# The factor of the norm ahead of an MLP, applied as its square behind the second matrix

## The chip, the core and the metric

The kernel runs on one core of a Trainium2 chip. The metric is the device time of one execution, in microseconds (us); lower is better. The engines are TensorE (PE; its weight loads are listed as PEld), VectorE (DVE), ScalarE (ACT), GpSimd (POOL) and SyncE (SP); the last two issue most of the DMAs here.

## The reference

One decoder layer on 16 meta tokens and 256 tokens of width 2048, all in fp32. The change works in the last third, the MLP, and what matters of it is:

```python
h = h + rms_norm(m @ w_o[l], g_post_mix[l])
u = rms_norm(h, g_pre_mlp[l])                           # h * r * g, r = rsqrt(mean(h*h) + eps) per token
f = jnp.square(jax.nn.relu(u @ w_up[l])) @ w_down[l]    # 2048 -> 8192 -> 2048
h = h + rms_norm(f, g_post_mlp[l])
```

The factor r is one positive number per token. It passes through the first matrix and the relu as a factor and through the square as its square. So f with r is f without r, times r*r, token by token.

## The kernel before

Ahead of the MLP come the mixers (some 500 us). The MLP starts at about 527 us of the span. A weight matrix is not multiplied as it is: each block of 128x2048 numbers ("raw") is cast by ScalarE to a coarser high part ("hi", line 1907), VectorE subtracts that from the block to get the low part ("lo", line 1912), and TensorE multiplies high by high, high by low and low by high. hi and lo stand in three buffers each, in turn, so the cast for a product can start when the product three places ahead of it has ended. Raw blocks come by DMA from SP's queue into seven places ("rooms").

The 8192 hidden columns are worked off in eight pieces. What TensorE does in a piece is a row of words written by hand:

- U0a0 to U1b1 are products with w_up (eight a piece, 32 matmuls each, in pairs of 512 and 256 columns; lines 551 and 557). The first digit is the half of the piece, the letter the pair of 128 columns in it, the last digit the half of the inner dimension. A pair ends in the PSUM banks u0 and u1, which every pair uses. A + means that the product belongs to the next piece.
- P1 to P7 and Q1 to Q7 are products with w_down (12 matmuls of 512 columns each, line 2082), in a scheme of seven products for eight blocks, on the left half of the output columns (P) and on the right one (Q). X1 to X4 are plain products in the last piece.
- R, in the first piece alone, stands for the broadcast of r: two fp32 matmuls of a matrix of ones with a diagonal (rows2, line 1969) give r along the free dimension, which VectorE copies to the tile rb.

After a pair of U products, up_pair reads the banks out (half on ScalarE, line 1980, the sum of halves on VectorE, line 1987, both 128x256). relu_squared then makes max(s, 0) * rb on VectorE (line 2007, 128x512), the square on ScalarE (line 2012), the sums of forms (lines 2023 to 2033) and their high and low parts (lines 2041 to 2059), which are the stationary side of the P and Q products. Work of piece 0 that needs rb waits in a list until R.

Some products want a sum of two w_down blocks (ADDS_FOR, eight a piece with forms). PIECE_SUMS says which of these VectorE adds up from two loaded blocks (line 1924, a 128x2048 addition, before the split). The others are "brought": POOL issues a DMA that adds the second block onto the first one in SBUF as it loads it (line 1929). There are 24 of the first kind and 36 of the second. give (line 2111) adds a finished P or Q product from its bank to the totals F and G.

The order of all other engines' work is set by a planner (Plan.order): TensorE's row is fixed, every other piece of work has a cost written by hand and gets a due time from the product that needs it, and each engine takes the work that is ready and due first. Each engine then runs its list in order.

At the end the sums of squares of the outputs are taken on ScalarE as the last columns come (square_of, line 1582, square_half, line 2361), end_norm makes the factor of the last norm, and finish_down multiplies, adds h and sends the result off:

```python
nc.scalar.activation(r, ssq, AF.Abs_reciprocal_sqrt, bias=v, scale=-4.0 / D)
minus4_mean(q, t, ssq)
between()
nc.vector.scalar_tensor_tensor(v, r, q, r, op0=ALU.mult, op1=ALU.mult)
nc.vector.scalar_tensor_tensor(r, v, 3.0, r, op0=ALU.add, op1=ALU.mult)
```

Of the kernel before, what the change touches and what calls it, by code (L numbers as in the profile page):

```python
# [213 lines left out]
def hybrid_block(ctx: ExitStack, tc: tile.TileContext, ins: dict, out: bass.AP):  # L214
# [1617 lines left out]
    products = [s for s in steps if s[0] != "R"]  # L1832
# [114 lines left out]
    r2 = const.tile([P, NT], F32, name="r2")  # L1947
    box2 = {}

    def mean2():  # L1950
        box2["v"] = v = tmp.tile([P, NT], F32, tag="tot", name="tot2")
        nc.vector.reduce_sum(v, ssq2, axis=mybir.AxisListType.X)
        nc.vector.tensor_scalar(v, v, 1.0 / D, RMS_EPS, op0=ALU.mult, op1=ALU.add)
# [12 lines left out]

    def rows2():
        for t in range(NT):
            nc.tensor.matmul(banks["b"][:, t * P:(t + 1) * P], ones, box2["diag"][t],
                             start=True, stop=True)  # L1970


    def up_pair(h, pr, i, accs, acc_names, s_name, s_tile):

        box = {}

        def half(j):
            def f():
                box[j] = tmp.tile([P, T], F32, tag="v", bufs=5, name=f"half_{h}{pr}{j}_{i}")
                nc.scalar.copy(box[j], accs[j][:, :T])  # L1980
            return f

        def total(j):
            def f():
                if j == 0:
                    box["s"] = s_tile().rearrange("p (j t) -> p j t", j=2)
                nc.vector.tensor_add(box["s"][:, j, :], box[j], accs[j][:, T:])  # L1987
# [12 lines left out]

    def relu_squared(h, pr, i, s_name, box):
# [3 lines left out]
        def relu():  # L2005
            s = box["s"]
            nc.vector.scalar_tensor_tensor(s, s, 0.0, rb[:, None, :T].broadcast_to([P, 2, T]),
                                           op0=ALU.max, op1=ALU.mult)
        plan.add("DVE", 0.66, relu, reads=(s_name, "rb"), writes=(s_name,), late=0.1)

        def square():
            nc.scalar.activation(box["s"], box["s"], AF.Square)
# [8 lines left out]
        plan.add("ACT", 0.53, square, reads=(s_name,), writes=(s_name,), late=0.1)  # L2021
# [279 lines left out]
    def end_norm(t, ssq, between=lambda: None):  # L2301
        v, q, r = norm3.v[:, t], norm3.q[:, t], norm3.r[:, t]
        nc.scalar.activation(r, ssq, AF.Abs_reciprocal_sqrt, bias=v, scale=-4.0 / D)
        minus4_mean(q, t, ssq)
        between()
        nc.vector.scalar_tensor_tensor(v, r, q, r, op0=ALU.mult, op1=ALU.mult)
        nc.vector.scalar_tensor_tensor(r, v, 3.0, r, op0=ALU.add, op1=ALU.mult)
# [48 lines left out]
    for e, (bank, cs) in enumerate(LAST_HALVES):  # L2356
        end_half("X4", 1, bank, cs)

        def square_half(e=e, bank=bank, cs=cs):
            junk = tmp.tile([P, CW], F32, tag="junk", bufs=1, name=f"sq_last_{e}")  # L2360
            nc.scalar.activation(junk[:, cs], banks[bank][:, cs], AF.Square,
# [49 lines left out]
```

## Time and profile before

| what | value |
|---|---|
| runs | 1173.03, 1175.72, 1176.04 us; median 1175.72 |
| the profiled execution | 1174.34 us, of which the span of instructions is 1172.6 |
| granted TensorE clock, mean | 0.998 |
| packets of POOL's DMA queue | 28.3% of 16 engines' span, 60.32 MB |
| moved in all | 296.36 MB, 253 GB/s |

The profile shows one execution. Busy times are per engine. The windows cut the span into stretches, here by the MLP's pieces. In a timeline, what stands in brackets is the engine's idle time ahead of the instruction and what ended it. A line number is one of the kernel before.

### The profile page before, as it was taken

The page shows a single profiled execution, that of the slowest core. Times are in us where ns is not written, and L with a number is a line of the kernel's source. Part 1 is how long each engine was busy: PE and PEld are TensorE (multiplying, and loading weights), DVE is VectorE, ACT ScalarE, POOL GpSimd, SP SyncE. Part 2 cuts the span into 40 slices and gives each one's busy share as a digit, 9 for nine tenths or more (in the row PEclk, how much of TensorE's full clock was granted, in tenths as well). Part 3 has the DMA queues.
Part 4 walks back from the last instruction along what each step waited for, and adds up shares of the span by engine and source line. Part 5 has one row for each costly group of instructions (what it writes and reads, how often), then busy time and mean ns, then how long its engine had stood idle before and what let it go on. Part 6 is the DMA issues. An engine that isn't in the chain of part 4 may idle for free.

```text
span 1172.6 us, 15841 instructions
## 1 busy us (share of the span) xinstructions
PE 1160.4 (99%) x6277; PEld 1006.5 (86%) x6277; DVE 1079.6 (92%) x1169; ACT 744.6 (64%) x748; POOL 77.8 (7%) x78
## 2 busy tenths in 40 slices
PE   9999999999999999999999999999999999999997
PEld 9999998888888888798888888888888888888886
DVE  6799999999999998788998998998999989989998
ACT  6745565566679655675775665665656655656655
POOL 1000000010000000000101001000000001010000
PEclk9999999999999999999999999999999999999999
DMA  9968776889978796668999999899998998998955
GB/s 295 263 211 220 161 230 208 262 249 265 309 195 271 217 356 182 216 224 282 264 309 231 249 309 257 236 311 236 288 287 227 326 248 240 329 260 240 325 144 179
DMA packets 193410, 296.36 MB, mean 253 GB/s; under 512 B 5065, under 2 KB 98953, under 8 KB 192552
## 3 DMA queue, kind: packets, MB, share of 16 engines
q1 hardware_dynamic: 161832, 234.31, 58.2%
q0 software_dynamic: 30896, 60.32, 28.3%
q8 instruction: 49, 0.80, 0.3%
q10 hardware_dynamic: 608, 0.73, 0.2%
q14 instruction: 25, 0.20, 0.0%
HBM read 291.14 MB, written 4.19 MB: 252 GB/s over the span
## 4 chain that ended last, share of the span: by engine, by line
PE 90%; DVE 6%; DMA 2%; issue 2%; ACT 1%; DVEq 0%; POOL 0%; ACTq 0%; POOLq 0%
PE bank_u L551 18%; PE bank_k L1331 12%; PE acc_up L2082 12%; PE bank_u L557 9%; PE bank_k L546 8%; PE acc_v L1331 8%; PE bank_a L2082 7%; PE bank_b L2082 6%; PE acc_v L546 4%; DVE lo L882 2%; DVE c L1019 1%; PE acc_up L551 1%; PE bank_k L1606 1%; DMA raw_p<-in_w_in_dram 1%; DMA raw_h<-in_w_down_dram 1%
## 5 line engine op out<-in xcount | busy, mean ns | idle before, releaser
L551 PE MATMUL bank_u<-m,hi 128*128 128x512 f32 x960 | 329.7, 390 | 0.2 <-DVE F_raw L1987 0.2
L557 PE MATMUL bank_u<-m,lo 128*128 128x256 f32 x960 | 265.4, 276 | 0.0
L551 PEld LDWEIGHTS bank_u<-m,hi 128*128 128x128 f32 x960 | 180.2, 188 | 38.4 <-DVE F_raw L1987 0.6
L1912 DVE TENSOR_TENSOR lo<-raw_m,hi 128x2048 fp32r<-128x2048 f32 x79 | 180.8, 2288 | 17.2 <-ACT hi L1907 16.3
L1907 ACT CAST hi<-raw_m 128x2048 fp32r<-128x2048 f32 x79 | 151.1, 1913 | 68.5 <-PE bank_u L551 48.5
L876 ACT CAST hi<-raw_p 128x2048 fp32r<-128x2048 f32 x73 | 139.3, 1912 | 78.3 <-PE bank_k L1331 17.1
L557 PEld LDWEIGHTS bank_u<-m,lo 128*128 128x128 f32 x960 | 180.3, 188 | 1.6
L882 DVE TENSOR_TENSOR lo<-raw_p,hi 128x2048 fp32r<-128x2048 f32 x70 | 159.5, 2283 | 12.8 <-ACT hi L876 12.7
L2082 PE MATMUL acc_up<-hi,forms 128*128 128x512 f32 (+1 forms) x456 | 146.9, 386 | 0.0
L1907 ACT CAST hi<-raw_h 128x2048 fp32r<-128x2048 f32 x42 | 80.3, 1913 | 38.5 <-PE bank_u L551 18.3
L1912 DVE TENSOR_TENSOR lo<-raw_h,hi 128x2048 fp32r<-128x2048 f32 x42 | 96.1, 2287 | 5.1 <-ACT hi L1907 4.7
L2082 PEld LDWEIGHTS acc_up<-hi,forms 128*128 128x128 f32 x456 | 85.2, 188 | 18.0 <-ACT G L2107 0.2
L1019 DVE SCALAR_TENSOR_TENSOR c<-a,taps,c 128x256 f32<-128x256 f32 x240 | 100.2, 475 | 0.0
L546 PE MATMUL bank_k<-u_um,hi 128*128 128x272 f32 x512 | 95.2, 287 | 0.0
L2082 PE MATMUL acc_up<-lo,forms 128*128 128x512 f32 (+1 forms) x228 | 88.2, 387 | 0.0
L2082 PE MATMUL bank_a<-hi,forms 128*128 128x512 f32 x256 | 84.1, 389 | 0.0
L546 PEld LDWEIGHTS bank_k<-u_um,hi 128*128 128x128 f32 x512 | 79.8, 188 | 0.0
L1331 PE MATMUL bank_k<-hi,u_um 128*128 128x512 f32 x248 | 79.1, 389 | 0.0
L546 PE MATMUL bank_k<-u_um,lo 128*128 128x272 f32 x256 | 73.3, 287 | 0.0
L1907 ACT CAST hi<-raw_c 128x2048 fp32r<-128x2048 f32 x23 | 43.9, 1908 | 39.2 <-PE bank_u L551 31.6
L2082 PE MATMUL bank_b<-hi,forms 128*128 128x512 f32 x192 | 63.1, 389 | 0.0
L1912 DVE TENSOR_TENSOR lo<-raw_c,hi 128x2048 fp32r<-128x2048 f32 x23 | 52.6, 2287 | 9.4 <-ACT hi L1907 9.3
(410 smaller groups left out, 2270.1 us busy)
## 6 DMA issues: line engine op xcount, KB each, us to landing
raw_p<-in_w_in_dram SPq DMA_DIRECT2D x31, 1024.0 KB, 6.5
raw_m<-in_w_down_dram SPq DMA_DIRECT2D x26, 1024.0 KB, 8.0
raw_m<-in_w_down_dram POOLq DMA_DIRECT2D x23, 1024.0 KB, 9.7
raw_h<-in_w_up_dram SPq DMA_DIRECT2D x18, 1024.0 KB, 7.8
raw_h<-in_w_down_dram SPq DMA_DIRECT2D x18, 1024.0 KB, 8.6
raw_m<-in_w_up_dram SPq DMA_DIRECT2D x17, 1024.0 KB, 8.1
raw_a<-in_w_up_dram SPq DMA_DIRECT2D x14, 1024.0 KB, 8.9
raw_c<-in_w_down_dram SPq DMA_DIRECT2D x14, 1024.0 KB, 5.8
```

What stands on the lines that cost most here:

```text
L546: nc.tensor.matmul(acc, w[:, k[0], cs], act[:, k[1], a, off:], start=first and n == 0, stop=last and n == 2)
L551: nc.tensor.matmul(acc.rearrange("p (a t) -> p a t", a=2)[:, :, ts], hi[:, k[0], cs], act[:, k[1], :, off + ts.start:off + ts.stop], start ...
L557: nc.tensor.matmul(acc[:, :T], lo[:, k[0], cs], act[:, k[1], 0, off:], start=False, stop=stop, skip_group_check=True)
L876: nc.scalar.copy(box["flat"][:, cs], rooms[q]()[:, cs])
L882: nc.vector.tensor_sub(lo[:, cs], rooms[q]()[:, cs], f32(box["flat"][:, cs]))
L1019: nc.vector.scalar_tensor_tensor(C_c()[:, q, :], A_a()[:, q, i:i + T], taps[:, q, i:i + 1], C_c()[:, q, :], op0=ALU.mult, op1=ALU.add)
L1331: nc.tensor.matmul(banks[bank], a_(k, part), box[w_][:, k, :], start=opens and k == 0 and i == 0, stop=ends_ and k == CK - 1 and i == 2, s ...
L1606: nc.tensor.matmul(acc, act(kk)(a_, half(t)), w_[:, k, :], start=kk == 0 and n == 0, stop=kk == nk - 1 and n == 2, skip_group_check=True)
L1907: nc.scalar.copy(box["flat"], raw_in(room))
L1912: nc.vector.tensor_sub(lo, raw_in(room), f32(box["flat"]))
L2082: nc.tensor.matmul(acc, forms[h][:, f, k, a_, :], box[w_][:, k, cs], start=start and k == 0 and n == 0, stop=stop and k == KH - 1 and n == ...
```

## The change

The factor r is no longer applied ahead of the square. Its square, rr2 = 1 / (mean + eps), one column per half of the tokens, is made in three small VectorE instructions. Relu and square are one VectorE instruction, max(s, 0) * s. rr2 comes in behind the second matrix: as the scale of the last squares and, through one ScalarE copy more, as a factor in end_norm. R, its diagonals, the root and the tile rb are gone. The rows of products and PIECE_SUMS are new; with them 30 of the block additions are on VectorE and 30 on POOL's queue: one more on VectorE in each of pieces 0 to 6 and one fewer in piece 7.

```diff
-PIECE_SUMS = ('P5 P6 Q4 Q5', 'P6 P7 Q5', 'P4 P5 P6', 'P5 P6')
-FIRST_PIECE = "U1a0 U1a1 R U1b0 U1b1 Q1 U0a0+ P1 U0a1+ P2 U0b0+ Q5 P5 Q7 P6 Q2 P3 P7 U0b1+ Q6 Q3 Q4 P4"
-PIECE = "U1a0 Q1 U1a1 U1b0 U1b1 P1 U0a0+ Q5 U0a1+ Q7 P5 Q3 P6 U0b0+ P3 Q6 P7 U0b1+ Q2 P2 P4 Q4"
-NEXT_TO_LAST = "U1a0 Q1 U1a1 U1b0 U1b1 P1 U0a0+ Q5 P5 U0a1+ Q7 P6 Q3 Q6 P3 U0b0+ P7 U0b1+ P2 Q4 P4 Q2"
-LAST_PIECE = "U1a0 U1a1 U1b0 U1b1 P1 X3 P5 X1 P3 P6 P2 P7 X2 X4 P4"
+PIECE_SUMS = ('P5 P6 Q4 Q6 Q7', 'P6 P7 Q4 Q5', 'P4 Q4 Q5 Q6', 'P5')
+FIRST_PIECE = "U1a0 U1a1 U1b0 U1b1 P1 Q1 U0a0+ Q7 U0a1+ P5 Q3 Q5 P6 U0b0+ P3 P7 Q6 U0b1+ Q2 Q4 P2 P4"
+PIECE = "U1a0 Q1 U1a1 P1 U1b0 U1b1 U0a0+ U0a1+ P5 Q5 P6 U0b0+ P3 P7 Q7 U0b1+ Q6 Q2 Q4 P2 P4 Q3"
+NEXT_TO_LAST = "Q1 P1 U1a0 U1a1 U1b0 U1b1 U0a0+ P5 Q5 Q3 U0a1+ Q6 Q2 P6 U0b0+ Q4 P3 P7 Q7 U0b1+ P2 P4"
+LAST_PIECE = "U1a0 U1a1 P1 U1b0 U1b1 X3 P5 X1 P3 P6 P2 P7 X2 X4 P4"
...
-    def root2():
...
-    def diag2():
...
-    def rows2():
-        for t in range(NT):
-            nc.tensor.matmul(banks["b"][:, t * P:(t + 1) * P], ones, box2["diag"][t],
-                             start=True, stop=True)
+    rr2 = const.tile([P, NT], F32, name="rr2")
+
+    def squared_norm2():
+        nc.vector.reduce_sum(rr2, ssq2, axis=mybir.AxisListType.X)
+        nc.vector.tensor_scalar(rr2, rr2, 1.0 / D, RMS_EPS, op0=ALU.mult, op1=ALU.add)
+        nc.vector.reciprocal(rr2, rr2)
...
-        def relu():
-            s = box["s"]
-            nc.vector.scalar_tensor_tensor(s, s, 0.0, rb[:, None, :T].broadcast_to([P, 2, T]),
+        def relu_square():
+            nc.vector.scalar_tensor_tensor(box["s"], box["s"], 0.0, box["s"],
                                            op0=ALU.max, op1=ALU.mult)
-        plan.add("DVE", 0.66, relu, reads=(s_name, "rb"), writes=(s_name,), late=0.1)
-        def square():
-            nc.scalar.activation(box["s"], box["s"], AF.Square)
...
-        plan.add("ACT", 0.53, square, reads=(s_name,), writes=(s_name,), late=0.1)
+        plan.add("DVE", 0.66, relu_square, reads=(s_name,), writes=(s_name,), late=0.1)
...
-        if s == "R":
-            plan.add("PE", 0.9, rows2, reads=("diag2",), writes=("b",))
-            plan.add("DVE", 0.4, lambda: nc.vector.tensor_copy(rb[:, :T], banks["b"][:, :T]),
-                     reads=("b",), writes=("rb",))
-            for rest in unscaled:
-                relu_squared(*rest)
-            continue
...
-        plan.add("ACT", 0.92, lambda: square_of(src, norm3.ssq, t, n), reads=(name,),
+        plan.add("ACT", 0.92, lambda: square_of(src, norm3.ssq, t, n, rr2[:, t:t + 1]),
+                 reads=(name, "rr2"),
...
     def end_norm(t, ssq, between=lambda: None):
         v, q, r = norm3.v[:, t], norm3.q[:, t], norm3.r[:, t]
         nc.scalar.activation(r, ssq, AF.Abs_reciprocal_sqrt, bias=v, scale=-4.0 / D)
+        nc.scalar.activation(ssq2[:, t, 0:1], r, AF.Copy, scale=rr2[:, t:t + 1])
         minus4_mean(q, t, ssq)
         between()
         nc.vector.scalar_tensor_tensor(v, r, q, r, op0=ALU.mult, op1=ALU.mult)
-        nc.vector.scalar_tensor_tensor(r, v, 3.0, r, op0=ALU.add, op1=ALU.mult)
+        nc.vector.scalar_tensor_tensor(r, v, 3.0, ssq2[:, t, 0:1],
+                                       op0=ALU.add, op1=ALU.mult)
...
-            nc.scalar.activation(junk[:, cs], banks[bank][:, cs], AF.Square,
+            nc.scalar.activation(junk[:, cs], banks[bank][:, cs], AF.Square, scale=rr2[:, 1:2],
```

Three places show how the order moves. The first is TensorE's row at the end of U1a1 and the start of U1b0 in piece 0 (bank_u0 and bank_u1 are the U banks, hi_n and lo_n the parts of the n-th block). Before:

```order
L557 MATMUL bank_u1_4513<-m_3529,lo_112_4499 128x256
L1969 MATMUL bank_b_4515<-diag2_0_4567,ones_91 128x128
L1969 MATMUL bank_b_4515<-diag2_1_4569,ones_91 128x128
L551 MATMUL bank_u0_4512<-m_3529,hi_113_4601 128x512
L557 MATMUL bank_u0_4512<-m_3529,lo_113_4605 128x256
```

After:

```order
L557 MATMUL bank_u1_4513<-m_3529,lo_112_4499 128x256
L551 MATMUL bank_u0_4512<-m_3529,hi_113_4595 128x512
L557 MATMUL bank_u0_4512<-m_3529,lo_113_4599 128x256
L551 MATMUL bank_u0_4512<-m_3529,hi_113_4595 128x512
L557 MATMUL bank_u0_4512<-m_3529,lo_113_4599 128x256
```

The two matmuls on ones are gone, and U1b0 follows U1a1 at once.

The second is VectorE in the middle of piece 2. Block lo_155 belongs to the first product of piece 2, so before lo_165, lo_166 and lo_167 are those of P5, Q3 and P6, and after lo_163, lo_164, lo_165 and lo_166 those of P5, Q5, P6 and U0b0. The rows TENSOR_TENSOR raw<-raw,raw are the sums of PIECE_SUMS. Before:

```order
L2111 TENSOR_TENSOR G_4506<-G_4506,acc_up00_3_4251 128x512
L2059 TENSOR_TENSOR forms_1_4504<-F_raw_4505,forms_1_4504 128x4x128
L1912 TENSOR_TENSOR lo_165_6122<-raw_m0_4509,hi_165_6099 128x2048
L2059 TENSOR_TENSOR forms_1_4504<-F_raw_4505,forms_1_4504 128x4x128
L1924 TENSOR_TENSOR raw_m0_4509<-raw_m0_4509,raw_m2_4511 128x2048
L1912 TENSOR_TENSOR lo_166_6142<-raw_c_4508,hi_166_6137 128x2048
L1987 TENSOR_TENSOR F_raw_4505<-half_000_3_6120,bank_u0_4512 128x256
L1912 TENSOR_TENSOR lo_167_6160<-raw_m0_4509,hi_167_6156 128x2048
L1987 TENSOR_TENSOR F_raw_4505<-half_001_3_6140,bank_u1_4513 128x256
```

After:

```order
L1912 TENSOR_TENSOR lo_163_6032<-raw_h1_4548,hi_163_6009 128x2048
L2030 TENSOR_TENSOR forms_0_4503<-F_raw_4505,forms_0_4503 128x4x128
L1924 TENSOR_TENSOR raw_h1_4548<-raw_h1_4548,raw_m1_4510 128x2048
L1912 TENSOR_TENSOR lo_164_6056<-raw_c_4508,hi_164_6054 128x2048
L2030 TENSOR_TENSOR forms_1_4504<-F_raw_4505,forms_1_4504 128x4x128
L2014 TENSOR_TENSOR forms_1_4504<-F_raw_4505,forms_1_4504 128x2x2x128
L2004 TENSOR_TENSOR F_raw_4505<-F_raw_4505 128x256
L1924 TENSOR_TENSOR raw_m0_4509<-raw_m0_4509,raw_m1_4510 128x2048
L1912 TENSOR_TENSOR lo_165_6110<-raw_h1_4548,hi_165_6091 128x2048
L1912 TENSOR_TENSOR lo_166_6114<-raw_h1_4548,hi_166_6112 128x2048
L1969 TENSOR_TENSOR F_raw_4505<-half_000_3_6074,bank_u0_4512 128x256
```

Before, one sum stands ahead of the split for Q3, and another follows further on. After, two sums stand within seven instructions, and the second one, for P7, is ahead of the splits for P6 and U0b0 and of the read-out of bank u0.

The third is ScalarE at the end, from the last but two of the sums of squares to the end of the second norm (ssq_mlp and last_ssq hold the sums, sq_last are the two halves of the last block). Before:

```order
L1582 ACTIVATE acking_offset=None)_2_1_9275,ssq_mlp_417<-acc_up00_1_4249 128x512
L2303 ACTIVATE r_mlp_420<-ssq_mlp_417,v_mlp_418 128x1
L2342 ACTIVATE raw_a_4507<-G_4506,r_mlp_420 128x512
L1582 ACTIVATE acking_offset=None)_0_1_9299,ssq_mlp_417<-bank_a_4514 128x512
L2361 ACTIVATE sq_last_0_9316,last_ssq_4517<-acc_up00_3_4251 128x256
L2361 ACTIVATE sq_last_1_9322,last_ssq_4517<-bank_u0_4512 128x256
L2303 ACTIVATE r_mlp_420<-last_ssq_4517,v_mlp_418 128x1
```

After:

```order
L1582 ACTIVATE acking_offset=None)_2_1_9229,ssq_mlp_417<-acc_up00_1_4249,rr2_4516 128x512
L2266 ACTIVATE r_mlp_420<-ssq_mlp_417,v_mlp_418 128x1
L2267 ACTIVATE ssq2_421<-r_mlp_420,rr2_4516 128x1
L2307 ACTIVATE raw_c_4508<-G_4506,r_mlp_420 128x512
L1582 ACTIVATE acking_offset=None)_0_1_9254,ssq_mlp_417<-bank_a_4514,rr2_4516 128x512
L2326 ACTIVATE sq_last_0_9271,last_ssq_4517<-acc_up00_3_4251,rr2_4516 128x256
L2326 ACTIVATE sq_last_1_9277,last_ssq_4517<-bank_u0_4512,rr2_4516 128x256
L2266 ACTIVATE r_mlp_420<-last_ssq_4517,v_mlp_418 128x1
L2267 ACTIVATE ssq2_421<-r_mlp_420,rr2_4516 128x1
```

Every square reads rr2 as its scale, and behind each of the two steps that make r_mlp stands a copy to ssq2 that multiplies it by rr2.

More of the change, by code (lines that the diff above doesn't have):

```diff
@@ L1831, in hybrid_block @@
         steps += [(s[:-1], i + 1) if s[-1] == "+" else (s, i) for s in text.split()]
-    products = [s for s in steps if s[0] != "R"]
+    products = steps
     def with_forms(i):
@@ L1944, in hybrid_block @@
     last_use_order = list(uses)
[L1947 to L1953, printed above, removed]
-    def root2():
-        box2["q"] = tmp.tile([P, NT], F32, tag="rs", bufs=1, name="rs_q_2")
-        nc.scalar.activation(box2["q"], box2["v"], AF.Sqrt)
-    def diag2():
-        rsqrt(r2, box2["q"], box2["v"])
-        box2["diag"] = []
-        for t in range(NT):
-            dg = tmp.tile([P, P], F32, tag="g", name=f"diag2_{t}")
-            nc.vector.tensor_scalar_mul(dg, ident, r2[:, t:t + 1])
-            box2["diag"].append(dg)
-    def rows2():
-        for t in range(NT):
-            nc.tensor.matmul(banks["b"][:, t * P:(t + 1) * P], ones, box2["diag"][t],
-                             start=True, stop=True)
+    rr2 = const.tile([P, NT], F32, name="rr2")
[3 more added lines that the diff above has]
+        nc.vector.reciprocal(rr2, rr2)
     def up_pair(h, pr, i, accs, acc_names, s_name, s_tile):
@@ L1992, in up_pair @@
                      late=0.1)
-        rest = (h, pr, i, s_name, box)
-        if "rb" in plan.writer:
-            relu_squared(*rest)
-        else:
-            unscaled.append(rest)
-    unscaled = []
+        relu_squared(h, pr, i, s_name, box)
     def relu_squared(h, pr, i, s_name, box):
@@ L2220, in hybrid_block @@
     loads()
-    plan.add("DVE", 0.4, mean2, reads=("ssq2",), writes=("v2",))
-    plan.add("ACT", 0.3, root2, reads=("v2",), writes=("q2",))
-    plan.add("DVE", 1.2, diag2, reads=("q2", "v2"), writes=("diag2",))
+    plan.add("DVE", 0.5, squared_norm2, reads=("ssq2",), writes=("rr2",))
     for pr in range(2):
@@ L2229, in hybrid_block @@
     for s, i in steps:
-        if s == "R":
-            plan.add("PE", 0.9, rows2, reads=("diag2",), writes=("b",))
-            plan.add("DVE", 0.4, lambda: nc.vector.tensor_copy(rb[:, :T], banks["b"][:, :T]),
-                     reads=("b",), writes=("rb",))
-            for rest in unscaled:
-                relu_squared(*rest)
-            continue
         for w in range(m_, min(m_ + 3, len(products))):
```

## The prediction

> **What bounds the kernel now.** I read the page's first table and its groups, then TensorE's own waits, then one window per piece of the MLP, then the timeline at the only MLP place where TensorE waited.
>
> ```profile
> PE 1160.4 (99%) x6277; PEld 1006.5 (86%) x6277; DVE 1079.6 (92%) x1169; ACT 744.6 (64%) x748; POOL 77.8 (7%) x78
> ...
> L1907 ACT CAST hi<-raw_m 128x2048 fp32r<-128x2048 f32 x79 | 151.1, 1913 | 68.5 <-PE bank_u L551 48.5
> ...
> PE ht L1674 <- issue: 2.0, 1, 2.0
> PE idle L460 <- POOL ident masks.py:199: 1.4, 1, 1.4
> PE bank_k L1331 <- DVE lo L882: 0.5, 1, 0.5
> PE bank_u L551 <- DVE F_raw L1987: 0.2, 1, 0.2
> ```
>
> TensorE is busy 99%, and of its named waits only the last, 0.2 us, lies in the MLP, where this change works. VectorE is second at 92%. ScalarE's casts of weights, 1.91 us each, wait mostly for TensorE (68.5 us of idle time before them), so TensorE sets their time and not they its. A busy TensorE need not be a TensorE at its pace, so the next view counts by pieces (columns: stretch, its length, busy time and instructions of PE, PEld, DVE, ACT, POOL, granted clock, DMA share, GB/s).
>
> ```profile
> 527.35:635.06 107.71, 107.47 (x570) 92.25 (x569) 96.41 (x89) 70.31 (x71) 7.70 (x6) 1.00 0.95 277
> ...
> 716.90:798.74 81.84, 81.84 (x426) 70.08 (x425) 75.38 (x64) 51.62 (x44) 6.42 (x5) 1.00 0.97 270
> ...
> 962.42:1044.26 81.84, 81.84 (x425) 70.08 (x425) 75.53 (x64) 51.49 (x44) 7.70 (x6) 1.00 1.00 278
> 1044.26:1123.34 79.08, 79.08 (x413) 67.93 (x413) 76.45 (x70) 50.23 (x44) 3.85 (x3) 1.00 0.87 256
> ```
>
> The five full pieces from 635.06 to 1044.26 are the same to 0.01 us, at full clock; the cuts are the starts of P1 (bank_a) in each: 8 U products of 5.46 us and 14 P and Q products of 2.72 us make 81.8. So TensorE runs there at its issue pace and nothing else sets the time. What the change can win on TensorE lies in the first window, before 635.06:
>
> ```profile
> 538.25 0.44 PE bank_b L1969 x4
> ...
> 616.51 2.29 DVE L1924 TENSOR_TENSOR raw_m<-raw_m,raw_h 128x2048 f32<-128x2048 f32 x1 [1.81 <-DMA raw_h<-in_w_down_dram]
> 618.72 2.28 DVE L1912 TENSOR_TENSOR lo<-raw_c,hi 128x2048 fp32r<-128x2048 f32 x1
> 620.92 2.29 DVE L1912 TENSOR_TENSOR lo<-raw_h,hi 128x2048 fp32r<-128x2048 f32 x1
> 623.12 0.41 DVE L1987 TENSOR_TENSOR F_raw<-half,bank_u 128x256 f32<-128x256 f32 x1
> ...
> 623.07 0.28 PE L557 MATMUL bank_u<-m,lo 128*128 128x256 f32 x1
> 623.59 0.50 PE L551 MATMUL bank_u<-m,hi 128*128 128x512 f32 x1 [0.24 <-DVE F_raw L1987]
> 623.93 0.28 PE L557 MATMUL bank_u<-m,lo 128*128 128x256 f32 x1
> ```
>
> First the broadcast of the norm's factor (L1969, 0.44 us of the chain). Then one late transfer: the sum at 616.51 waited 1.81 us for it, two splits stood behind the sum, and the bank of U1a1 was read out only at 623.12, when U1b0 wanted it.
>
> **The change, part by part.** *Broadcast gone.* The two fp32 matmuls on ones leave TensorE's row: -0.44 us, fully, since TensorE's row is the path. VectorE's and ScalarE's little steps around them (root, Newton, two diagonals, copy to rb) lie off the path: nothing.
>
> *The stall at 623.* From 623.07 the next matmul starts 0.52 us later instead of 0.11 (-0.41), and the one after 0.34 instead of 0.23 (-0.11). Behind the stall pairs come 0.35 us apart, before it 0.34:
>
> ```profile
> 535.53 0.23 PE bank_u L551
> ...
> 535.87 0.23 PE bank_u L551
> ...
> 624.21 0.23 PE bank_u L551
> 624.56 0.23 PE bank_u L551
> ...
> 635.06 2.75 PE bank_a L2082 x12
> ```
>
> That holds for 31 pairs, from 624.21 to 635.06 (-0.31). In the new row P1 stands between U1a1 and U1b0 in piece 1, so the bank has 2.72 us more; the stall of this place should go, all 0.83 us. If a new one like it comes, the gain is 0.
>
> *Square moved.* The rows of the work that changes hands:
>
> ```profile
> L2007 DVE SCALAR_TENSOR_TENSOR F_raw<-F_raw,rb 128x512 f32<-128x512 f32 x32 | 21.9, 688 | 0.5
> L2012 ACT ACTIVATE F_raw<-F_raw 128x512 f32<-128x512 f32 x32 | 20.0, 629 | 3.3 <-DVE F_raw L2007 3.2
> L1924 DVE TENSOR_TENSOR raw_m<-raw_m,raw_h 128x2048 f32<-128x2048 f32 x10 | 22.8, 2284 | 1.8 <-DMA raw_h<-in_w_down_dram 1.8
> ...
> raw_m<-in_w_down_dram POOLq DMA_DIRECT2D x23, 1024.0 KB, 9.7
> ```
>
> VectorE's instruction stays one of 128x512 with two inputs, 0.69 us; that the second input is now the tile itself I cost at nothing, shape and inputs being alike. Were it doubled, four of 0.69 us a piece and the sum below would still lie under the 6.46 us that VectorE has free. ScalarE loses 32 x 0.63 = 20.0 us, and the way from a U product to its forms loses 0.63 us and a hop. ScalarE is busy 51.6 of 81.84 us a piece, so the 20 us are worth nothing themselves.
>
> *Sums.* The eight additions of blocks were 24 on VectorE and 36 as accumulating transfers; now 30 and 30. Six transfers of 1 MB leave POOL's queue. VectorE gets one sum more in each of pieces 0 to 6 and one fewer in piece 7. A 2.28-us instruction holds VectorE for 2.20 us (the next starts 2.20 later, below). A middle piece goes from 75.38 to 77.58 of 81.84 us, 94.8%: it fits, if each split still arrives in time. How near it was, by VectorE's and TensorE's timelines of the same piece:
>
> ```profile
> 733.18 2.29 DVE L1924 TENSOR_TENSOR raw_m<-raw_m,raw_m 128x2048 f32<-128x2048 f32 x1
> 735.38 2.29 DVE L1912 TENSOR_TENSOR lo<-raw_c,hi 128x2048 fp32r<-128x2048 f32 x1
> ...
> 738.83 0.39 PE L2082 MATMUL acc_up<-lo,forms 128*128 128x512 f32 x1
> ...
> 754.20 0.68 DVE L2111 TENSOR_TENSOR F_raw<-F_raw,bank_b 128x512 f32<-128x512 f32 x1
> 754.80 2.28 DVE L1912 TENSOR_TENSOR lo<-raw_h,hi 128x2048 fp32r<-128x2048 f32 x1
> ...
> 757.92 0.28 PE L557 MATMUL bank_u<-m,lo 128*128 128x256 f32 x1
> ```
>
> The split behind a sum ends at 737.67 and is first used at 738.83: 1.16 us to spare. The tightest, behind a bank's read-out, ends at 757.08 and is used at 757.92: 0.84. It must be so: the buffers are three, so a cast starts when the product three places ahead ends, and two P or Q products (5.44 us) have to cover cast (1.91) and split (2.28).
>
> Now the new middle row at its densest, the sum for P7 ahead of the split for P6 (lo_165). Time 0 is the start of U0a1; P5, Q5, P6, U0b0 start at 5.44, 8.16, 10.88, 13.60. lo_164 waits for its cast until 2.0 and holds VectorE to 4.2; two forms (0.60 each) and a 256-wide step (0.41) to 5.8; the sum to 8.0; lo_165 to 10.2 and some 0.1 to its end, wanted at 10.88 + 0.23 = 11.11: 0.8 us to spare. lo_166 goes to 12.4, and the bank's read-out behind it (0.41) ends at 12.8, wanted at 13.60: 0.8. In the run of six, Q6 Q2 Q4 P2 P4 Q3, the same counting gives 0.85 at Q3, and 0.4 at P1 where NEXT_TO_LAST prolongs the run by Q1 P1. Each is positive, so the sums cost 0. Bounds: 0, and 2.20 - 0.84 = 1.36 us a piece where one stands uncovered, over seven pieces 9.5. I take 0, as the sum at 733.18 shows one right ahead of a tight split without a stall.
>
> *New rows of products.* The products are the same in number and kind, so TensorE's own time is unchanged. In PIECE the pair U1b1 U0a0 stands unseparated where U1a1 U1b0 did: one such place each.
>
> *The end.* Ten squares now take their scale from a column, and end_norm has one ScalarE step more. Nearest rows:
>
> ```profile
> 1157.00 0.63 ACT L1582 ACTIVATE ng_offset=None)_1_1_9256<-F_raw 128x512 f32<-128x512 f32 x1
> 1159.04 0.20 ACT L2292 ACTIVATE r_mlp<-ones 128x1 f32<-128x1 f32 x1
> 1160.48 0.72 ACT L2342 ACTIVATE raw_a<-G,r_mlp 128x512 f32<-128x512 f32 x1 [0.48 <-DVE r_mlp L2307]
> 1164.59 0.38 ACT L2361 ACTIVATE sq_last<-bank_u 128x256 f32<-128x256 f32 x1 [0.96 <-PE bank_u L2082]
> 1165.10 0.29 ACT L2303 ACTIVATE r_mlp<-last_ssq,v_mlp 128x1 f32<-128x1 f32 x1
> 1165.51 0.21 DVE L2306 SCALAR_TENSOR_TENSOR v_mlp<-r_mlp,q_mlp 128x1 f32<-128x1 f32 x1
> 1165.75 0.16 DVE L2307 SCALAR_TENSOR_TENSOR r_mlp<-v_mlp,r_mlp 128x1 f32<-128x1 f32 x1
> ```
>
> A scale from a column costs 0.72 - 0.63 = 0.09 us. The last square (1164.59) is on the path: +0.09. The new copy of one column (0.20) runs from 1165.39 to 1165.59 beside VectorE's step at 1165.51 and is wanted at 1165.75, with a hop of 0.12 (1165.39 to 1165.51) in between at 1165.71: hidden by 0.04. Bounds 0 to 0.3; I take +0.1.
>
> *Sum.* -0.44 - 0.83 + 0.1 = -1.17 us. The profiled execution took 1174.34 us (span 1172.6 and 1.74 around it), so it would take 1173.2. The median of the runs is 1.38 above it; the mean of the four executions shown is 1174.8, which puts the forecast at **1173.6**.
>
> **The rivals.** *VectorE becomes the bound (slower).* If the margins that I counted are short, every piece overdraws; from 0.7 us in each of seven pieces the total passes +0.3%, and with a sum wholly uncovered it is 9.5 - 1.2 over the profiled execution: 1182.6. For it: 0.4 us at one place, 94.8%. Against: the count above, and pieces at 75.38 us that show no wait. [...] The trace so far does not call VectorE saturated, with 6.46 us free a piece.
>
> *Another late transfer.* A sum in VectorE's row waits for both operands; a transfer that lands late holds all splits behind it, as at 616.51, where 1.81 us became 0.83 on TensorE. With a sum more in each of the crowded pieces 0 and 1, one to three such stalls give 1174.4 to 1176.1. Against: six fewer accumulating transfers (9.7 us to landing) in a DMA system at a share of 0.95 to 1.00.
>
> *The end takes it back.* With the copy fully on the path and hops, +0.5: 1174.1.
>
> *The gain does not come.* TensorE waits for the next thing where L1969 stood, or the stall at 623 stays: 1174.8, no change.
>
> *More than counted (faster).* Relief of ScalarE and DMA would have to shorten something that sets the time; the equal 81.84 us of five pieces leave 1.3 us in all. [...] Faster by 3.5 us needs scatter of the runs.
>
> **How the numbers follow.** 0.3% (3.5 us) is about what a measurement of this kernel can tell from no change; the three runs lie 3.0 us apart. Chances: the forecast with the two small rivals (end, no gain) 0.75, late transfers 0.13 (0.03 of it slower), VectorE 0.07, more 0.05. Faster 0.06 (with a little scatter), slower 0.10, same 0.84. The range runs from the lowest run less all of 1.4 us, 1171.6, to the highest less 1.2 plus three small stalls, 1177.4; only the VectorE rival and the tails lie outside.
>
> **What would show it.** Right: no L1969 on the chain, middle pieces of 81.84 us with VectorE at about 77.6, ScalarE's total near 725, POOL's queue with 30 additions, TensorE without a wait near 623. Wrong: a stretch over 81.84 between equal products, TensorE waits for lo or for F_raw that repeat in each piece, or a sum with a wait for a transfer in front of a late U product.

## The result, and the profile after

The changed kernel takes 1176.37 us (median of 22 runs, 1174.41 to 1179.34), the kernel before 1174.87 (22 runs, 1172.71 to 1176.2). The ratio is 1.0013, with a 95% interval of 1.0008 to 1.0019: slower by 1.5 us. That is within the 0.3% that were called no change, and on the other side of before than the forecast of 1173.6. The profiled execution took 1176.33 us, its span 1174.6.

Most of what the prediction counted is there. The first line is of the page's first table, the others are windows from the start of U1a0 of one piece to that of the next (columns as in the prediction):

```profile
PE 1159.7 (99%) x6273; PEld 1006.7 (86%) x6273; DVE 1091.7 (93%) x1168; ACT 729.4 (62%) x717; POOL 70.1 (6%) x72
```

```profile
527.72:612.24 84.52, 82.39 (x426) 70.35 (x425) 77.69 (x68) 54.43 (x52) 3.88 (x3) 1.00 0.88 267
612.24:694.04 81.80, 81.80 (x426) 70.10 (x425) 76.97 (x65) 49.98 (x41) 5.10 (x4) 1.00 0.89 254
694.04:775.84 81.80, 81.80 (x426) 70.07 (x425) 77.55 (x66) 49.55 (x40) 5.13 (x4) 1.00 0.91 259
...
857.64:939.44 81.80, 81.80 (x426) 70.06 (x425) 77.59 (x66) 49.59 (x40) 5.13 (x4) 1.00 0.90 257
```

Pieces 1 to 4 last 81.80 us, with TensorE busy for all of it and VectorE for 77.0 to 77.6 of it. The piece that was disturbed before (the stall at 623) is now as short as the others. But the first window, piece 0, is 2.72 us longer than its neighbours, and its TensorE is 2.13 us short of filling it. TensorE's waits name the place:

```profile
PE ht L1674 <- issue: 2.4, 1, 2.4
PE bank_u L551 <- DVE F_raw L1969: 2.1, 1, 2.1
```

The second line is new. (Line numbers are those of the changed kernel: half is now made at 1962, the total of the halves at 1969, relu and square at 1982, the copies of forms at 1994, the casts of forms at 2012 and 2028, P and Q products at 2053.) TensorE's timeline shows where it stands:

```profile
538.28 0.39 PE L551 MATMUL bank_u<-m,hi 128*128 128x512 f32 x1
538.50 0.28 PE L557 MATMUL bank_u<-m,lo 128*128 128x256 f32 x1
540.91 0.50 PE L551 MATMUL bank_u<-m,hi 128*128 128x512 f32 x1 [2.13 <-DVE F_raw L1969]
541.24 0.28 PE L557 MATMUL bank_u<-m,lo 128*128 128x256 f32 x1
```

The last matmul of U1a1 starts at 538.50, the first of U1b0 at 540.91, where R stood before. U1b0 writes the banks of U1a and has to wait until they are read out. From one matmul to the next that is 2.41 us in place of 0.11. The two products behind it, U1b0 and U1b1, take 5.70 and 5.60 us in place of 5.44 each, so the wait and the slower products behind it make up the whole 2.72 us. Why the read-out was late is on ScalarE's timeline of the changed kernel:

```profile
526.47 0.90 ACT L1962 COPY half<-acc_up 128x256 f32<-128x256 f32 x3
529.61 0.62 ACT L2012 CAST forms<-F_raw 128x512 fp32r<-128x512 f32 x1 [2.24 <-DVE F_raw L1982]
530.14 0.40 ACT L1994 COPY F_raw<-F_raw 128x256 f32<-128x256 f32 x1
530.45 1.91 ACT L1907 CAST hi<-raw_a 128x2048 fp32r<-128x2048 f32 x1
532.25 0.36 ACT L1962 COPY half<-acc_up 128x256 f32<-128x256 f32 x1
535.77 0.62 ACT L2012 CAST forms<-F_raw 128x512 fp32r<-128x512 f32 x1 [3.15 <-DVE F_raw L1982]
536.29 1.90 ACT L1907 CAST hi<-raw_c 128x2048 fp32r<-128x2048 f32 x1
538.10 0.61 ACT L2028 CAST forms<-F_raw 128x512 fp32r<-128x512 f32 x1
538.62 0.36 ACT L1962 COPY half<-bank_u 128x256 f32<-128x256 f32 x1
```

The same stretch of ScalarE in the kernel before:

```profile
527.39 1.91 ACT L1907 CAST hi<-raw_a 128x2048 fp32r<-128x2048 f32 x1
529.20 0.37 ACT L1980 COPY half<-acc_up 128x256 f32<-128x256 f32 x1
532.73 1.91 ACT L1907 CAST hi<-raw_c 128x2048 fp32r<-128x2048 f32 x1 [3.16 <-PE bank_u L551]
535.56 0.37 ACT L1980 COPY half<-bank_u 128x256 f32<-128x256 f32 x1 [0.93 <-PE bank_u L557]
```

Before, the casts of weights for U1b0 (hi_113, from raw_a) and U1b1 (hi_114, from raw_c) came first, since forms of piece 0 could not be made until R had given rb. Now relu needs no rb. The first relu starts at 528.88, 1.2 us after U1a0; before, it started 12.3 us after U1a0. The planner therefore has the first cast of a form ready early and puts it ahead of hi_113. ScalarE works its list in order: it stands for 2.24 us in front of a form that VectorE has not made, and hi_113 runs at 530.45 in place of 527.39. VectorE's timeline carries the delay on, split, total, relu, then over ScalarE's next form to hi_114, its split, and only then the total that frees U1a's bank:

```profile
528.88 0.69 DVE L1982 SCALAR_TENSOR_TENSOR F_raw<-F_raw 128x512 f32<-128x512 f32 x1
...
532.38 2.29 DVE L1912 TENSOR_TENSOR lo<-raw_a,hi 128x2048 fp32r<-128x2048 f32 x1 [1.41 <-ACT hi L1907]
534.59 0.41 DVE L1969 TENSOR_TENSOR F_raw<-half,acc_up 128x256 f32<-128x256 f32 x1
535.04 0.69 DVE L1982 SCALAR_TENSOR_TENSOR F_raw<-F_raw 128x512 f32<-128x512 f32 x1
...
538.23 2.29 DVE L1912 TENSOR_TENSOR lo<-raw_c,hi 128x2048 fp32r<-128x2048 f32 x1 [1.11 <-ACT hi L1907]
540.44 0.41 DVE L1969 TENSOR_TENSOR F_raw<-half,bank_u 128x256 f32<-128x256 f32 x1
```

The same total, and the first relu behind it, on VectorE's timeline of the kernel before:

```profile
536.88 0.41 DVE L1987 TENSOR_TENSOR F_raw<-half,bank_u 128x256 f32<-128x256 f32 x1
...
539.48 1.29 DVE L2007 SCALAR_TENSOR_TENSOR F_raw<-F_raw,rb 128x512 f32<-128x512 f32 x2
```

At this point it was a reading of the trace. The experiments had to show that the order of ScalarE's list causes the wait, and that the wait is the whole loss.

### The profile page after: what moved, and what is told of

Its sections match the earlier page's. It is cut to its first block, busy times and chain, and to the rows that moved or that the text cites. A ratio compares the mean times of both kernels' runs of the same rounds, so it can differ in the third digit from the quotient of the medians.

```text
span 1174.6 us, 15790 instructions
## 1 busy us (share of the span) xinstructions
PE 1159.7 (99%) x6273; PEld 1006.7 (86%) x6273; DVE 1091.7 (93%) x1168; ACT 729.4 (62%) x717; POOL 70.1 (6%) x72
## 4 chain that ended last, share of the span: by engine, by line
PE 96%; DVE 1%; DMA 1%; issue 1%; ACT 1%; ACTq 0%; DVEq 0%; SPq 0%
PE bank_u L551 18%; PE bank_k L1331 17%; PE acc_up L2053 13%; PE acc_v L1331 10%; PE bank_u L557 9%; PE bank_k L546 8%; PE bank_a L2053 7%; PE bank_b L2053 6%; PE acc_v L546 4%; PE bank_k L1606 1%; DMA raw<-in_w_up_dram 1%; PE acc_up L551 1%; ACT hi L1907 0%; DMA raw<-in_w_in_dram 0%; PE bank_y L1442 0%
## 5 line engine op out<-in xcount | busy, mean ns | idle before, releaser
L1907 ACT CAST hi<-raw_m 128x2048 fp32r<-128x2048 f32 x72 | 137.8, 1913 | 73.0 <-PE bank_u L551 28.0
L1912 DVE TENSOR_TENSOR lo<-raw_m,hi 128x2048 fp32r<-128x2048 f32 x72 | 164.6, 2288 | 10.0 <-ACT hi L1907 9.3
L1907 ACT CAST hi<-raw_h 128x2048 fp32r<-128x2048 f32 x48 | 91.9, 1914 | 56.2 <-PE bank_u L551 38.1
L1912 DVE TENSOR_TENSOR lo<-raw_h,hi 128x2048 fp32r<-128x2048 f32 x48 | 109.8, 2287 | 6.7 <-ACT hi L1907 6.4
L1907 ACT CAST hi<-raw_a 128x2048 fp32r<-128x2048 f32 x23 | 44.0, 1913 | 25.8 <-PE bank_u L551 13.7
```

The lines of the kernel that those rows point to most:

```text
L1907: nc.scalar.copy(box["flat"], raw_in(room))
L1912: nc.vector.tensor_sub(lo, raw_in(room), f32(box["flat"]))
```

## The experiments

Theory A: ScalarE's list in piece 0. Theory B: the new rows and the six more sums on VectorE. Theory C: the end. Theory D, formed after the first runs: a wait of this size comes there whatever ScalarE's order. Each ratio is to runs of the kernel before that were taken beside it (medians 1174.87 to 1174.96). The stretch in the table runs from the start of the first matmul of U1a0 in piece 0 to the start of the last matmul, in the profiled execution; it leaves out what differs from run to run ahead of the MLP (U1a0 starts between 526.3 and 529.3 us). The slot is U1a1 of piece 0, from its start to that of U1b0; 5.44 without a wait.

| kernel | median, us | ratio to before (95%) | stretch, us | slot, us |
|---|---|---|---|---|
| before | 1174.9 | 1 | 637.02 | 5.80 (R in it) |
| changed | 1176.37 | 1.0013 (1.0008 to 1.0019) | 638.20 | 7.73 |
| weights' casts ahead of forms' casts | 1175.16 | 1.0003 (0.9995 to 1.0012) | 638.08 | 7.57 |
| the same, ahead of the copies too | 1172.73 | 0.9984 (0.9975 to 0.9993) | 635.50 | 5.44 |
| planner knows VectorE's first 4.0 us | 1173.55 | 0.9987 (0.9978 to 0.9995) | 635.48 | 5.44 |
| relu of U0a, U0b held until U1a1 | 1174.6 | 0.9999 (0.999 to 1.0008) | 636.79 | 5.44 |
| first form's cast four times | 1179.3 | 1.0049 (1.0035 to 1.0064) | 641.46 | 9.40 |
| new computation, old rows and sums | 1224.5 | 1.0428 (1.041 to 1.0447) | 685.10 | 7.17 |
| old computation, new rows and sums | 1187.32 | 1.0107 (1.0094 to 1.012) | 648.48 | 5.80 (R in it) |
| new computation and rows, old sums | 1244.5 | 1.0591 (1.0577 to 1.0605) | 706.38 | 7.59 |

### Weights' casts ahead of the forms' casts

```diff
-        plan.add("ACT", 0.6, lambda: nc.scalar.copy(dst(0), src()), reads=(s_name,), writes=(A,),
-                 late=0.1)
+        gate = tuple(half_names(w)[0] for w in (2, 3)) if i == 0 and h == 0 else ()
+        plan.add("ACT", 0.6, lambda: nc.scalar.copy(dst(0), src()), reads=(s_name,) + gate,
+                 writes=(A,), late=0.1)
```

(The read-outs of U0a and U0b are entered into the plan after U1a0, so that the names of both casts exist.)

> The changed kernel with one difference: in piece 0 ScalarE's two casts of weights hi_113 and hi_114 stand ahead of the casts of the forms made from U0a and U0b, as they did before the change; from hi_116 on every row of ScalarE and VectorE is the changed kernel's. Theory A (ScalarE's order in piece 0 is the cause: hi_113 waits behind a form that is not yet there, so the bank of U1a is read out late and TensorE waits 2.3 us at U1b0): the wait at U1b0 is gone, 1174.9 - 0.4 (broadcast) - 0.8 (stall of before at 623) + 0.3 (end) = 1173.9, ratio to before 0.999. Theory B (the new rows and the six more sums on VectorE cost the time): as the changed kernel, 1176.4, ratio 1.0013. Theory C (the end, scale from a column and copy): 1176.4 too, the 1.5 us behind the last product.

Measured: 1175.16 us, and the wait stayed, with a slot of 7.57. Taken alone this speaks against theory A. ScalarE's timeline says why it doesn't:

```profile
530.22 0.41 ACT L1994 COPY F_raw<-F_raw 128x256 f32<-128x256 f32 x1 [2.28 <-issue]
530.53 1.90 ACT L1907 CAST hi<-raw_a 128x2048 fp32r<-128x2048 f32 x1
...
535.85 0.41 ACT L1994 COPY F_raw<-F_raw 128x256 f32<-128x256 f32 x1 [3.15 <-DVE F_raw L1982]
536.16 1.90 ACT L1907 CAST hi<-raw_c 128x2048 fp32r<-128x2048 f32 x1
```

The casts were moved back, but the copies of the same forms (L1994), which wait for the same relu, took their place ahead of hi_113 and hi_114, with the same two waits. The experiment moved the wrong half of what waits. Its stretch is 0.12 us shorter than the changed kernel's; the 1.2 us between the medians are not explained by it, and the two intervals overlap.

### The copies moved too

```diff
-                     reads=(s_name,), writes=(f"q1{pr}",), late=0.1)
+                     reads=(s_name,) + gate, writes=(f"q1{pr}",), late=0.1)
```

> The kernel with the two casts of weights ahead of the forms' casts, and now ahead of the two copies (sources of the sums of forms) too, which wait for the same relu. Theory A (any instruction of ScalarE's list that waits for relu and stands ahead of hi_113 or hi_114 holds the read-out of U1a): the 2.1 us at U1b0 are gone, from the start of U1a0 to the last matmul 635.5 us in place of 638.1, median 1173.6, ratio 0.9987. Theory D (the casts' order is not it): U1b0 still waits about 2 us, 1175.2.

Measured: 1172.73 us, slot 5.44, stretch 635.50. Taking the copies out of the way as well removes the wait and 2.58 us of the stretch. No form stands ahead of hi_113 or hi_114 now, as in the kernel before. VectorE's list is the same in this kernel and the last one up to and beyond the total that frees U1a's bank, and TensorE's row and the orders of both DMA queues are the same throughout. So the place of the two copies in ScalarE's list alone decided about the wait.

### The planner told the truth about VectorE

```diff
+    plan.add("DVE", 4.0, lambda: None, writes=("F0", "F1"))
     for pr in range(2):
         up_done(0, pr, 0, accs[2 * pr:2 * pr + 2], [f"x{pr}{j}" for j in range(2)])
```

> The changed kernel; the planner alone is told that VectorE is taken for the first 4.0 us of its plan, which on the chip it is. No instruction is added. The plan then puts ScalarE's cast hi_113 ahead of the first form's cast and copy, in place of behind them; those and three places of VectorE's list in piece 0 are the only difference. Theory A (an instruction of ScalarE's list that waits for relu stands ahead of hi_113 and so delays the read-out of U1a): no wait of TensorE at U1b0 of piece 0; 1176.4 - 2.7 = 1173.7, or 1174.9 - 0.44 - 0.83 + 0.17 (end as measured) = 1173.8, ratio to before 0.999. Theory B (new rows, six more sums on VectorE): 1176.4. Theory D (a wait of that size comes there anyway, from the transfer of in_w_up that lands at 523 or from another instruction): the wait at U1b0 stays over 1 us, 1175.5 to 1176.4.

Measured: 1173.55 us. No instruction was added, and none beyond ScalarE's and VectorE's lists in piece 0 moved. TensorE's waits, all of them:

```profile
PE ht L1674 <- issue: 2.4, 1, 2.4
PE idle L460 <- POOL ident masks.py:199: 1.4, 1, 1.4
```

and ScalarE's timeline, where hi_113 now waits only for its buffer:

```profile
527.82 1.91 ACT L1907 CAST hi<-raw_a 128x2048 fp32r<-128x2048 f32 x1 [0.81 <-PE acc_up L551]
529.63 0.37 ACT L1962 COPY half<-acc_up 128x256 f32<-128x256 f32 x1
529.89 0.63 ACT L2012 CAST forms<-F_raw 128x512 fp32r<-128x512 f32 x1
```

So the form's cast and copy behind hi_113 cost nothing, the same two ahead of it 2.72 us (638.20 less 635.48). This also says why the plan was wrong. The planner starts with all engines empty. On the chip VectorE still had the last split of the first products to make, since a transfer of w_up had landed late (ScalarE's cast for it waited until 523.28), and was free for the MLP only at 527.43; TensorE's row in the plan begins four steps of 1.36 us ahead of U1a0, thus at 522.3. VectorE's late start is then 5.1 us into the plan; the 4.0 us that the planner is told here are enough to turn the order. As the planner took the form first, its plan must have had the form ready before hi_113's buffer was free. On the chip it was the other way round: the form was ready at 529.61, and hi_113's buffer at about 527.9 (0.2 us after U1a0, as in this kernel and in the one before), 1.7 us earlier.

### Relu of U0a and U0b held until U1a1

```diff
+        gate = ("u1",) if i == 0 and h == 0 else ()
-        plan.add("DVE", 0.66, relu_square, reads=(s_name,), writes=(s_name,), late=0.1)
+        plan.add("DVE", 0.66, relu_square, reads=(s_name,) + gate, writes=(s_name,), late=0.1)
```

(and the work behind it is entered into the plan after U1a1.)

> The changed kernel with the release of relu and square of U0a and U0b in piece 0 put off, in the plan only, until U1a1 has run, as the broadcast did before the change. ScalarE's list is then that of before up to hi_115: both casts of weights, then both halves of U1a, then forms. Theory A: no wait at U1b0, 1173.8, ratio 0.999, as the kernel in which the planner knows VectorE's first 4.0 us. Theory B: 1176.4. Theory D: the wait stays, 1175.5 to 1176.4.

Measured: 1174.6 us; the slot is 5.44, as theory A says, but the stretch is 1.31 us longer than the two kernels above. The new loss is one wait at the end of piece 0:

```profile
594.74 0.40 PE L551 MATMUL bank_u<-m,hi 128*128 128x512 f32 x1
595.98 0.39 PE L557 MATMUL bank_u<-m,lo 128*128 128x256 f32 x1 [0.84 <-DVE lo L1912]
```

On VectorE a sum (L1924, 591.43 to 593.64) stands ahead of that split in this kernel and behind it in the one where the planner knows VectorE's state. A sum ahead of a tight split is what the prediction's VectorE rival was about. It exists, and at this one place it costs about 1 us.

### The form's cast four times

```diff
+        def cast():
+            for _ in range(4 if (i, h, pr) == (0, 0, 0) else 1):
+                nc.scalar.copy(dst(0), src())
-        plan.add("ACT", 0.6, lambda: nc.scalar.copy(dst(0), src()), reads=(s_name,), writes=(A,),
+        plan.add("ACT", 0.6, cast, reads=(s_name,), writes=(A,),
```

> The changed kernel with the first cast of a form in piece 0 written four times in place of once (the same values, three more ScalarE instructions of 0.62 us ahead of hi_113); all other rows as they are. Theory A: TensorE's wait at U1b0 grows by the whole 1.9 us, from 2.3 to 4.2: 1178.3. Theory B and theory C: 1.9 us of ScalarE, which is busy 62%, disappear: 1176.4.

Measured: 1179.3 us, 2.9 above the changed kernel: more than theory A, far from B and C. The slot grew by 1.67 us (9.40 less 7.73). The four casts took 1.96 us more, and ScalarE began them 0.28 us earlier against TensorE than in the changed kernel: 1.68. The rest is a thing that no theory had: the product behind the wait took 7.25 us in place of 5.70. Windows of that product and of the next:

```profile
542.36:549.61 7.25, 7.25 (x32) 6.30 (x33) 7.18 (x9) 1.07 (x2) 0.00 (x0) 0.76 0.71 247
549.61:555.00 5.39, 5.39 (x33) 4.76 (x32) 3.10 (x3) 2.28 (x2) 0.73 (x1) 1.00 0.02 8
```

The granted clock is 0.76 in the first and 1.00 in the second. The last section comes back to it.

### New computation with the old rows, old computation with the new rows

The first takes rows and PIECE_SUMS of before without R, the second adds R, rb and the separate square to the new rows and sums.

> The changed computation (factor behind the second matrix, relu and square in one instruction) with the rows of products and the sums of before. ScalarE's order up to hi_114 is the changed kernel's. Theory A: TensorE waits 2 to 3 us at U1b0 of piece 0, 1174.9 - 0.4 + 2.7 + 0.3 = 1177.4, or 1176.6 if the stall at the start of U1b0 of piece 1 does not come back. Theory B: 1174.9 - 0.4 + 0.3 = 1174.7. Theory C: 1176.4 with no wait of TensorE in piece 0.

> The computation of before (broadcast of the factor, relu and square apart) with the new rows of products and the new choice of sums. Theory A: no wait at U1b0 of piece 0, the stall of before at 623 gone: 1174.9 - 0.8 = 1174.0, ratio 0.9993. Theory B: slower than before as the changed kernel is, 1176 to 1177. Theory C: 1174.0 as theory A.

Measured: 1224.5 and 1187.32 us. No theory had either. The wait that A expects in piece 0 is there in the first (slot 7.17; the wait is 1.6 us, A expected 2 to 3) and not in the second (5.80 with R in it, as before), and both carry far larger waits elsewhere. TensorE's waits of the first:

```profile
PE acc_up L2053 <- ACT forms L2028: 14.6, 6, 2.4
PE acc_up L2053 <- DVE forms L2030: 7.4, 6, 1.5
```

One of the six, on ScalarE's and TensorE's timelines:

```profile
645.22 1.90 ACT L1907 CAST hi<-raw_h 128x2048 fp32r<-128x2048 f32 x1 [1.77 <-PE bank_u L551]
647.02 1.65 ACT L2028 CAST forms<-F_raw 128x512 fp32r<-128x512 f32 x3
```

```profile
647.69 0.79 PE L2053 MATMUL acc_up<-hi,forms 128*128 128x512 f32 x1 [2.44 <-ACT forms L2028]
```

It is the same pattern with the parts exchanged: the form that TensorE's next product needs stands behind a cast of weights which itself waits for TensorE to finish a product. Every piece from 1 to 6 takes 88.5 to 88.8 us in place of 81.84. In the second kernel the largest wait is 2.4 us for a total that frees a bank (L1987); by the same cuts its piece 0, with R in it, takes 86.53 us and its piece 6 81.73, where the changed kernel's rows without a wait take 81.80 and 76.32.

So the rows do not fit the one computation better than the other in general. They fit the lists that the planner makes from them, and the two halves of the change can't be priced apart by undoing one. For theory B this pair of runs is not a test, though it was meant as one; the kernel with the planner told of VectorE is, since it keeps new rows and sums and is faster than before.

### New computation and rows, old sums

```diff
-PIECE_SUMS = ('P5 P6 Q4 Q6 Q7', 'P6 P7 Q4 Q5', 'P4 Q4 Q5 Q6', 'P5')
+PIECE_SUMS = ('P5 P6 Q4 Q5', 'P6 P7 Q5', 'P4 P5 P6', 'P5 P6')
```

In the new rows Q7 comes ahead of Q5 in piece 0, so with the old choice Q5's sum takes a block onto which another has been added already: some values of the sums change.

> The changed computation and the new rows with the old choice of sums: 24 on VectorE and 36 as accumulating transfers. ScalarE's list up to hi_116 is the changed kernel's. Theory A: the same wait at U1b0 (2.3 us); the sums cost nothing, 1176.4, unless transfers land late: then waits of VectorE's sums or of TensorE for lo in the crowded pieces, and slower. Theory B: the six more sums were the cost: faster than the changed kernel by 1 to 2 us, 1174.9.

Measured: 1244.5 us; the slot has the same wait as the changed kernel (7.59), and the rest of theory A's clause, slower by waits elsewhere, came at 68 us. The choice of sums belongs to the rows as well, and fewer sums on VectorE made nothing faster.

### The end without column scale and copy

```diff
-        nc.scalar.activation(ssq2[:, t, 0:1], r, AF.Copy, scale=rr2[:, t:t + 1])
...
-        nc.vector.scalar_tensor_tensor(r, v, 3.0, ssq2[:, t, 0:1],
-                                       op0=ALU.add, op1=ALU.mult)
+        nc.vector.scalar_tensor_tensor(r, v, 3.0, r, op0=ALU.add, op1=ALU.mult)
...
-            nc.scalar.activation(junk[:, cs], banks[bank][:, cs], AF.Square, scale=rr2[:, 1:2],
+            nc.scalar.activation(junk[:, cs], banks[bank][:, cs], AF.Square,
```

> The kernel in which the planner knows VectorE's first 4.0 us, without the scale of the last two squares and without the copy of one column in the norm's end: the last norm leaves the factor of the norm ahead of the MLP out, so its values change; the instructions are otherwise the same. If the end costs what its rows say (0.09 for the scale, 0.08 for the copy, behind which the last step waits): from the start of the last matmul to the last step on r_mlp 1.54 us as before the change, in place of 1.70. If the copy is hidden: 1.61.

Measured: 1173.51 us in its one run, and from the last matmul (1163.46) to the last step on r_mlp 1.55 us:

```profile
1164.76 0.21 DVE L2270 SCALAR_TENSOR_TENSOR v_mlp<-r_mlp,q_mlp 128x1 f32<-128x1 f32 x1
1165.01 0.16 DVE L2271 SCALAR_TENSOR_TENSOR r_mlp<-v_mlp,r_mlp 128x1 f32<-128x1 f32 x1
```

With scale and copy (the changed kernel, last matmul at 1165.92) it is 1.71:

```profile
1166.30 0.47 ACT L2326 ACTIVATE sq_last<-bank_u,rr 128x256 f32<-128x256 f32 x1 [0.87 <-PE bank_u L2053]
...
1167.22 0.29 ACT L2267 ACTIVATE ssq<-r_mlp,rr 128x1 f32<-128x1 f32 x1
```

```profile
1167.31 0.21 DVE L2270 SCALAR_TENSOR_TENSOR v_mlp<-r_mlp,q_mlp 128x1 f32<-128x1 f32 x1
1167.63 0.16 DVE L2271 SCALAR_TENSOR_TENSOR r_mlp<-v_mlp,ssq 128x1 f32<-128x1 f32 x1
```

The end costs 0.16 us. Theory C is out.

## Why the prediction was wrong, step by step

| term | predicted, us | measured, us |
|---|---|---|
| broadcast gone | -0.44 | -0.45 |
| stall at 623 gone | -0.83 | -0.83 |
| sums, new rows | 0 | 0 with these lists; -0.2 over five pieces, cause not shown |
| end | +0.1 | +0.16 |
| TensorE's wait at U1b0 of piece 0 | not in the sum | +2.72 |

The measured terms are of the profiled executions, the first two from the kernel without the wait in which the planner knows VectorE's state: its slots of U1a1 and U1b0 are 5.44 and 5.44 us, before 5.80 and 5.53 (-0.45); its piece 1 takes 81.80 us, before 82.67 (-0.87, of which 0.04 is what each other piece lost too).

**What bounds the kernel**: right. TensorE's pace sets the middle pieces, 81.80 us, and VectorE stands at 77.6 as forecast; ScalarE's total is 729.4 (near 725 was forecast). POOL's busy time fell from 77.8 to 70.1 us.

**Broadcast gone**: this step failed. "-0.44 us, fully, since TensorE's row is the path" holds only if what comes behind R in the row is ready when R is no longer there. In the same breath the step called VectorE's and ScalarE's work around R "off the path: nothing". But R also held back the work of relu and its forms in piece 0. With R gone that work is released up to 11 us earlier (the first relu 1.2 us after the start of U1a0 in place of 12.3), lands in ScalarE's list in front of two casts of weights, and these are on the way to the read-out of U1a. The prediction followed the instructions that were removed, and not those that the removed wait had held. The order of ScalarE's list in piece 0 could be read beforehand; the prediction looked at TensorE's row and at VectorE's margins only.

**Square moved**: the sizes were right (VectorE's instruction 0.69 us in both kernels, ScalarE's total 744.6 before and 729.4 now), and no run contradicts "worth nothing". Whether the shorter way to the forms adds to the harm in piece 0 is not shown, since no run takes it apart from the release of relu.

**The stall at 623**: right, it is gone and no late transfer replaced it.

**Sums**: right for the lists of this kernel, by the margins counted. The kernel with relu held shows the other case, one sum ahead of one tight split, at 1.0 to 1.3 us; the upper bound given was 1.36 a place.

**The end**: 0.16 for 0.1. The last square cost its 0.09 as counted; the copy was not hidden. It took 0.29 us, not the 0.20 of the row that was taken as nearest: it has a column operand, as the square has (+0.09), and as the step of 0.29 us at 1165.10 has, which the prediction showed too; so the last step waits for it by 0.08 instead of finding it done 0.04 ahead. (Nine squares take the scale, not ten; the sum uses the last one alone.)

**The rivals**: the one that came true is "The gain does not come", with "TensorE waits for the next thing where L1969 stood". Its place was exact and its price was not: it was put at no change, as if the wait could at most fill the gap that R left. This wait, 2.13 us, was not bounded by the gap, 0.36 us (the slot: 5.80 us with R in it, 5.44 without). On the profiled executions: forecast 1173.17, measured 1176.33; of the 3.16 between, 2.72 is the wait, 0.53 is that U1a0 started later in this execution (527.72 for 527.19, within what differs from run to run there), 0.18 the end with the transfers behind it, less 0.27 that the rest of the MLP was faster than counted. VectorE, at 93%, does not set the time of pieces 1 to 4: they hold 81.80 us of matmuls in 81.80 us and show no wait of TensorE that less work on VectorE could shorten.

With the wait mended, the forecast and its sum hold: 1173.55 and 1172.73 us, for 1173.6, and terms of -1.3 us for -1.17. That the first of the two comes within 0.05 us is luck: the runs of that kernel lie up to 2.5 us apart, and the 0.8 us between the two medians are not in their stretches, which are equal to 0.02 us.

## What to carry to other kernels

When a wait is removed, list what it was holding back, and find where that work now stands in each engine's list: work that comes free early can stand in front of something that matters and wait there for a third engine. In a kernel whose lists are made by a planner, a row of products fits the lists that come of it and nothing else, so a part undone is no measure of that part; change the list alone instead. And tell such a planner what the engines are still busy with when it starts; here 4.0 us of VectorE were worth 2.7 us.

## What the hardware showed

ScalarE did not pass an instruction that waited: in the changed kernel it stood idle for 2.24 us ahead of a form's cast, while the next but one, hi_113, had all it needed from about 527.9 (as the kernel that runs it at that point shows).

A wait of TensorE can cost more than its length. In the kernel with four casts, after 3.79 us of idling, matmuls of 512 and 256 columns started about 0.64 us apart per pair in place of 0.34 for five pairs, and then went on at 0.35. In the kernel with the old sums two waits for the read-out of a bank, each of 1.87 us, end at 645.24 and at 833.46. Behind the first, pairs started 0.64 us apart for five pairs; behind the second, 0.35. Windows behind the two:

```profile
645.20:649.00 3.80, 3.76 (x13) 3.24 (x14) 3.80 (x3) 0.62 (x1) 0.00 (x0) 0.55 0.83 265
...
833.50:838.00 4.50, 4.50 (x25) 3.94 (x26) 4.50 (x3) 1.75 (x2) 0.00 (x0) 1.00 0.64 204
```

The granted clock is 0.55 in the one and 1.00 in the other. The wait of 2.13 us in the changed kernel was not followed by the slow pace: from 540.91 to 546.61 pairs start 0.35 us apart, and the granted clock is 1.00. This also goes some way to say why the kernels with many waits lost so much: with the old rows the two lines of waits shown come to 22 us, three smaller ones in the MLP to 6, and the stretch grew by 48. The mean granted clock of that execution is 0.978, of the changed kernel's 0.996, and over the changed kernel's stretch it is 1.00. The 0.018 between the two means, of a span of 1222.4 us, is some 22 us, an estimate, which is about the difference.

The slow pace can be seen in the changed kernel as well, ahead of the MLP, behind the wait of 2.44 us in front of L1674, which ends at 498.40: the granted clock is 1.00 from 498.50 to 499.40, 0.50 from 499.52 to 502.90 and 1.00 from 503.00 to 508.00. So it lasted about 3.4 us there. If the clock falls to 0.50 in the kernels with four casts and with the old sums too, their windows, 0.76 over 7.25 us and 0.55 over 3.80 us, come to 3.5 and 3.4 us, an estimate.

What decides whether a wait is followed by it is not shown. Its length alone does not: of the two waits of 1.87 us one was followed by it and one was not, and the longer one of 2.13 us was not.
